# The product of a normalised tile's sum with a row, in two steps of 512 columns, with the power to -1/2 issued between them

## The chip, the cores and the metric

The kernel runs on one core of a Trainium2 chip. Its engines run side by side, each through a list of instructions of its own in order: PE multiplies matrices (PEld is its weight load), ACT evaluates functions and copies, DVE and POOL work element by element, SP and POOL also issue DMAs. The metric is the device time of one execution in microseconds (us), from timed runs; the median of three runs of the kernel before is 1109.74 us.

## What is computed

The reference is a backbone of two layers over 512 tokens of width 1024. Layer 0 is windowed attention over 16 heads with 256 context tokens, layer 1 a chunked gMLP; each is followed by a SwiGLU network with 2816 hidden columns. Both sub-layers are wrapped in the same way, and that wrapping is where the change lies:

```
def rmsnorm(x, g):
    y = x * rsqrt(mean(x * x, axis=-1) + 1e-6)
    return y * g

def modulate(h, shift, scale):
    return h * (1 + scale) + shift

h = modulate(rmsnorm(x, norm_g[i, 0]), sh_m, sc_m)
y = mixer_i(h)                                   # attention (i = 0) or gMLP (i = 1)
x = x + g_m * rmsnorm(y, norm_g[i, 1])
f = swiglu(modulate(rmsnorm(x, norm_g[i, 2]), sh_f, sc_f))
x = x + g_f * rmsnorm(f, norm_g[i, 3])
```

The last two lines of one sub-layer and the first of the next are one piece of work for each tile of 128 tokens: normalise the product y, add it to x, normalise the new x, scale and shift it, and turn it so that the next product can take it as an operand.

## The kernel before

All of x (512 tokens) stays in SBUF as four tiles of 128 tokens; c0, c1, c2 and c3 below are these tiles and the objects that carry them (`Chain`). A product in full precision is three matmuls: each operand is split into a high part (a cast on ACT, L216) and a low part (a subtraction on DVE, L223).

`down` (L1193 on) is a **seam**: it finishes the product of one sub-layer for the four tiles in turn and starts the next sub-layer's product (its head). There are three seams of this kind. Seam 1 lies between attention and the first SwiGLU network (about 255 to 300 us of the profile), seam 2 between that network and the gMLP (600 to 640), seam 3 between the gMLP and the second network (745 to 790). In seam 1 the tiles c2 and c3 carry a part of the sum in SBUF (`y_part`), so `merge` adds it, and their `gain_y` reads SBUF alone.

For each tile the steps are, with engine and line of the profile:

| step | what it does | engine, line |
|---|---|---|
| square_y, rstd_y | mean square of y; add 1e-6 on DVE, power to -1/2 on POOL (`ry`) | ACT L243, DVE L252/L250, POOL L253 |
| gain_y | tmp = y * G | DVE L1149 |
| add_x | x = tmp * ry + x, 1024 columns | DVE L1153 |
| square_x, rstd_x | mean square of x; the power of it (`rx`) | ACT L243, DVE L250, POOL L253 |
| gain_x | right half of tmp = x * row, 1024 columns | POOL L1165 |
| shift_x z | tmp = tmp * rx + row, 512 columns, z = 0, 1 | DVE L1169 |
| turn z | four transposes of 128x128 into PSUM (`hT`) | PE L1176 |
| turned_hi, turned_lo | high and low part of the turned half, into H | ACT L216, DVE L223 |

Right behind the transposes PE runs the head's matmuls (`fa` at seams 1 and 3, `v` at seam 2). In seams 1 and 3 POOL also computes sums of weights (`T`, L1408) and DVE sums of activations (`a_sum`, L1377) that the SwiGLU network needs a little later.

**What sets the order.** Every step is registered by `at(time, step, ...)`. `run_plan` sorts the steps by their place in the table ORDER (L41 to L199), a list of step names, and calls them in that order, which fixes the order of the instructions on each engine's queue. A step that is not in the table is placed by its `time`. So a change of the table moves instructions, and an engine whose next instruction has to wait holds back all that stands behind it in its list.

`rstd_of` (L247) is a DVE addition followed by the power on POOL; POOL executes it in its own order, so a power that stands behind a gain_x waits for it.

Of the kernel before, what the change touches and what calls it, by code (L numbers as in the profile page):

```python
# [11 lines left out]
ALU = mybir.AluOpType  # L12
# [3 lines left out]
D = 1024  # L16
# [25 lines left out]
x_fetch_5 x_fetch_4 square_in_4 x_fetch_1 warm_0 rstd_in_4 warm_1 dma dma#2 square_in_5 square_in_1 warm_2 warm_3  # L42
rstd_in_5 wfetch_0_0 rstd_in_1 x_fetch_2 norm_in_4_0 norm_in_5_1 norm_in_1_0 turn_in_4_0 square_in_2 norm_in_1_1
turn_in_1_0 warm_4 x_fetch_0 x_fetch_3 square_in_0 turn_in_5_1 norm_in_5_0 rstd_in_2 norm_in_2_0 turn_in_5_0
ada0_fetch_0 turned_in_4_0 square_in_3 rstd_in_0 turn_in_1_1 turned_in_5_0 turned_in_1_0 ada0_rows_0 turn_in_2_0
# [3 lines left out]
wlow_0_0 turned_in_2_0 ada0_fetch_4 ada0_cols_1 turned_in_0_0 turned_in_3_0 ada0_rows_2 modulate0_0 wfetch_1 dma#5  # L49
kv_0_4 modulated_high_0 turned_in_2_1 ada0_rows_out_2 modulated_low_0 ada0_cols_2 kv_0_2 dma#4 kv_0_3 ada0_done_1  # L50
modulated_high_1 modulate0_ctx_1 kv_0_5 ada0_done_2 modulate0_1 modulated_ctx_1 whigh_0_1 modulated_low_1 ada0_fetch_6
ada0_rows_3 norm_in_4_1 turn_in_4_1 m2start ada0_rows_out_3 turned_in_4_1 modulate0_ctx_2 kv_1_2 kv_1_4 kv_1_5
turned_in_0_1 modulated_high_2 ada0_cols_3 modulate0_2 modulated_ctx_2 kv_0_0 modulated_low_2 ada0_fetch_5 whigh_1_0
wlow_0_1 ada0_rows_4 wfetch_2 wlow_1_0 whigh_1_1 ada0_done_3 kv_1_3 kv_2_4 ada0_fetch_7 kv_2_5 modulate0_3
ada0_rows_out_4 modulated_high_3 kv_1_0 kv_0_1 kv_2_3 kv_1_1 modulate0_ctx_3 modulated_ctx_3 ada0_cols_4 ada0_done_4
modulated_high_4 ada0_rows_6 kv_3_4 wlow_1_1 ada0_rows_5 modulated_low_3 ada0_rows_out_5 m2fetch_0 modulate0_ctx_4
modulated_ctx_4 kv_2_0 kv_2_2 m2fetch_1 ada0_cols_5 modulate0_4 <lambda>#2 ada0_done_5 kv_3_2 modulated_low_4
whigh_2_0 kv_2_1 kv_3_0 ada0_rows_out_6 kv_3_5 kv_4_0 m2fetch_2 ada0_cols_6 modulated_high_5 kv_4_4 ada0_rows_7
wlow_2_0 ada0_rows_out_7 modulate0_ctx_5 whigh_2_1 kv_3_3 kv_3_1 modulate0_5 ada0_done_6 kv_4_3 m2add_0 q_first_0_0_0
m2add_1 q_first_0_0_1 kv_4_1 modulated_low_5 kv_4_2 kv_4_5 ada0_cols_7 wlow_2_1 modulate0_6 q_first_0_0_2 m2fetch_3  # L60
kv_5_2 modulated_high_6 modulated_low_6 kv_5_0 modulated_ctx_5 kv_6_2 q_first_0_0_3 q_first_0_0_4 dma#3 ada0_done_7
modulate0_7 q_first_0_0_5 kv_5_3 kv_5_1 m2add_2 kv_6_0 modulated_high_7 kv_5_4 kv_5_5 m2add_3 kv_6_1 modulate0_ctx_6
m2add_4 modulated_low_7 m2add_5 modulated_ctx_6 q_first_0_0_6 kv_7_0 modulate0_ctx_7 modulated_ctx_7 kv_6_3 kv_7_1
kv_7_2 wfetch_3 kv_7_3 kv_6_4 q_first_0_0_7 q_first_0_1_0 kv_6_5 q_first_0_1_1 q_first_0_1_2 kv_7_4 m2add_6
q_first_0_1_3 q_first_0_1_4 q_first_0_1_5 m2add_7 k_copy_0 q_first_0_1_6 m2fold q_first_0_1_7 q_first_1_0_0 v_copy_0
k_copy_2 table_Exp kv_7_5 k_rope_2 whigh_3_0 q_first_1_0_1 q_first_1_0_2 k_rope_0 m2mirror v_copy_4 k_add_2
q_first_1_0_3 k_turn_2 q_first_1_0_4 q_first_1_0_5 k_add_0 wlow_3_0_0_512 k_copy_4 k_turn_0 q_first_1_0_6
q_first_rows_0 k_split_2_0 v_copy_2 wlow_3_0_512_1024 whigh_3_1 q_next_q_mults_0 q_first_1_0_7 q_first_1_1_0
k_split_0_0 <lambda>_0 wlow_3_1_0_512 wlow_3_1_512_1024 q_next_q_split_0 q_first_1_1_1 k_turn_4 q_first_1_1_2
q_first_1_1_3 k_split_0_1 q_first_1_1_4 q_first_1_1_5 q_first_1_1_6 q_turns_0_0_bankA k_split_4_0 q_first_1_1_7  # L70
k_split_2_1 q_turns_0_1_bankA q_copy_0_0 q_first_rows_1 k_split_4_1 q_copy_0_1 block_0 q_step_2_0 q_step_2_1
q_step_2_2 m4fetch_0 score_0_0 q_step_2_3 bound_0_0 exp_0_0 score_0_1 q_step_2_4 m2fetch_gain score_0_2 q_step_2_5
bound_0_1 score_0_3 q_step_2_6 q_step_2_7 exp_0_1 q_next_q_mults_1 block_1 score_1_0 bound_0_2 bound_0_3 exp_0_2
<lambda>_1 exp_0_3 sink_0 bound_1_0 m4start total_0 q_step_2_8 q_step_2_9 score_1_1 normalise_0_3 wfetch_4 q_step_2_10
bound_1_1 q_step_2_11 q_step_2_12 q_next_q_split_1 score_1_2 q_turns_1_0_bank_t block_2 bound_1_2 score_1_3 m3start
normalise_0_1 exp_1_0 exp_1_1 q_step_2_13 q_step_2_14 bound_1_3 q_step_2_15 q_turns_1_1_bank_t q_copy_1_0 score_2_1
q_step_3_0 normalise_0_2 m4add_0 exp_1_2 q_next_q_rows_2 q_step_3_1 block_3 whigh_4_0 exp_1_3 q_step_3_2 normalise_0_0
turn_0_0 q_step_3_3 q_step_3_4 score_2_0 wlow_4_0_0_512 q_step_3_5 wfetch_5 turn_0_1 sink_1 q_copy_1_1 q_step_3_6
q_step_3_7 q_next_q_mults_2 q_step_3_8 score_2_2 total_1 turn_0_2 m2stack q_step_3_9 bound_2_1 bound_2_0 q_step_3_10
# [123 lines left out]
def backbone_kernel(ctx: ExitStack, tc: tile.TileContext, a, out):  # L203
    nc = tc.nc
# [416 lines left out]
    for t in range(NT):  # L621
        b = (3.6, 5, 6.5, 8)[t]
# [4 lines left out]
        for h in range(2):  # L627
            b = (6.4, 7.9, 9.5, 11)[t] + .45 * h
# [1426 lines left out]
```

## Time and profile before

| what | value |
|---|---|
| median of the three timed runs | 1109.74 us (1109.18 to 1111.7) |
| the profiled execution's own time | 1110.8 us |
| its span, first to last instruction | 1109.0 us |
| granted clock of TensorE | 0.998 of full |
| PEld busy | 954.6 us (86%) |
| DVE busy | 946.9 us (85%) |
| ACT busy | 613.7 us (55%) |
| POOL busy | 256.7 us (23%) |
| DVE busy in 270 to 280, 280 to 290, 290 to 300 us (seam 1) | 9.92, 9.51, 9.33 us of 10 |
| POOL busy in the same stretches | 7.58, 7.90, 9.61 us of 10 |

In rows of the timeline the columns are the start in us, the duration in us, engine, line, operation, output and inputs with their shapes, the count of instructions merged into the row, and in brackets how long the engine had stood idle before and what ended that. The duration of a row runs from when the engine takes the instruction to its end, so it holds a wait for something that the engine needs inside the instruction. The rows of waits give, for an instruction and what released it, the sum in us, how often, and the longest.

### The profile page before, as it was taken

Reading aid. Unit: us, or ns where it says so; the run is one execution under the profiler, and the core shown is the slowest. Engines: PE = TensorE matmul, PEld = TensorE weight load, DVE = VectorE, ACT = ScalarE, POOL = GpSimd, SP = SyncE. Lnnn points to the kernel's source line nnn. Section 1 sums busy time; section 2 is a strip of 40 time slices with the busy share of each in tenths; the row PEclk is TensorE's granted clock in tenths of the full one; section 3 lists DMA queues with packets and bytes.
Section 4 is the critical chain, followed back from the end, with each engine's and each line's share of the span. In section 5 each row is a group of like instructions: output and inputs, shape, how many; then the busy total and the mean of one; then the engine's idle time right before and its main releaser. Section 6 shows DMA issues by size and latency. Waiting matters only on the chain.

```text
span 1109.0 us, 17873 instructions
## 1 busy us (share of the span) xinstructions
PE 1087.6 (98%) x6974; PEld 954.6 (86%) x6974; DVE 946.9 (85%) x1418; ACT 613.7 (55%) x1060; POOL 256.7 (23%) x276
## 2 busy tenths in 40 slices
PE   7999999999999999999999999999999999999997
PEld 4688877778899999998888788888999999998876
DVE  5788988968999999987987777878988888879985
ACT  6456678756655555545665534337555545546652
POOL 1516585533700000001320511006400000002400
PEclk9999999999999999999999999999999999999999
DMA  9642433143245646449963296662133343369911
GB/s 360 266 151 89 169 95 115 64 147 114 85 151 183 210 163 198 170 136 319 239 125 116 74 330 227 203 203 82 68 132 126 134 152 123 126 223 319 167 32 76
DMA packets 48856, 179.15 MB, mean 162 GB/s; under 512 B 4858, under 2 KB 9210, under 8 KB 37636
## 3 DMA queue, kind: packets, MB, share of 16 engines
q1 hardware_dynamic: 41220, 163.34, 42.4%
q0 software_dynamic: 7552, 14.68, 7.7%
q8 instruction: 54, 0.88, 0.3%
q14 instruction: 30, 0.25, 0.1%
HBM read 171.71 MB, written 2.10 MB: 157 GB/s over the span
## 4 chain that ended last, share of the span: by engine, by line
PE 86%; DVE 7%; POOL 2%; issue 2%; DMA 1%; ACT 1%; SPq 0%; DVEq 0%; POOLq 0%; ACTq 0%
PE f L1448 35%; PE y L1632 13%; PE y L280 7%; PE y L1659 4%; PE v L280 4%; PE o_ps L957 3%; PE s_ps L904 3%; PE pT_ps L937 2%; PE u L1868 1%; PE u L1866 1%; PE u L1867 1%; DVE w_lo L223 1%; PE q_ps L272 1%; PE q_ps L274 1%; PE q_ps L273 1%
## 5 line engine op out<-in xcount | busy, mean ns | idle before, releaser
L1448 PE MATMUL f<-H,w_hi 128*128 128x256 f32 x960 | 178.6, 284 | 1.1 <-DVE fc L1459 0.5
L1448 PEld LDWEIGHTS f<-H,w_hi 128*128 128x128 f32 x960 | 149.7, 192 | 2.3 <-DVE fc L1459 1.4
L1448 PE MATMUL f<-H,w_lo 128*128 128x256 f32 x480 | 135.8, 283 | 0.0
L1632 PE MATMUL y<-w_hi,s 128*128 128x512 f32 x448 | 120.1, 389 | 0.0
L1448 PE MATMUL f<-S,w_hi 128*128 128x256 f32 x640 | 118.6, 283 | 0.0
L216 ACT CAST w_hi<-w_raw 128x1024 fp32r<-128x1024 f32 x90 | 94.6, 1053 | 34.9 <-PE y L1632 11.9
L216 ACT CAST w_hi<-T 128x1024 fp32r<-128x1024 f32 x80 | 83.6, 1047 | 52.4 <-PE f L1448 33.7
L1455 ACT COPY fc<-f 128x256 f32<-128x256 f32 x120 | 44.8, 373 | 105.7 <-PE f L1448 102.6
L223 DVE TENSOR_TENSOR w_lo<-w_raw,w_hi 128x1024 fp32r<-128x1024 f32 (+1 forms) x81 | 96.4, 1195 | 6.7 <-ACT w_hi L216 6.7
L1448 PEld LDWEIGHTS f<-S,w_hi 128*128 128x128 f32 x640 | 99.9, 192 | 0.0
L1632 PEld LDWEIGHTS y<-w_hi,s 128*128 128x128 f32 x448 | 84.1, 188 | 17.4
L223 DVE TENSOR_TENSOR w_lo<-T,w_hi 128x1024 fp32r<-128x1024 f32 x80 | 97.3, 1217 | 0.0
L1448 PEld LDWEIGHTS f<-H,w_lo 128*128 128x128 f32 x480 | 92.1, 192 | 0.0
L1448 PE MATMUL f<-S,w_lo 128*128 128x256 f32 x320 | 90.7, 284 | 0.5 <-DVE w_lo L223 0.5
L1620 POOL DMA_DIRECT2D t<-in_w x48 | 42.3, 939 | 184.3 <-DMA t<-in_w 117.2
L396 POOL DMA_DIRECT2D acc<-acc x8 | 6.9, 865 | 312.6 <-DVE acc L382 308.8
L382 DVE SCALAR_TENSOR_TENSOR acc<-ada_k,sc,acc 128x1024 f32<-128x1024 f32 x56 | 71.6, 1279 | 8.6 <-DMA ada_k<-in_ada 6.6
L1632 PE MATMUL y<-w_lo,s 128*128 128x512 f32 x224 | 69.1, 390 | 0.6 <-DVE w_lo L223 0.6
L1448 PE MATMUL f<-H,x 128*128 128x256 f32 x480 | 64.3, 283 | 0.0
L931 POOL TENSOR_SCALAR p<-p,st 128x512 f32<-128x512 f32 (+1 forms) x64 | 53.3, 848 | 43.8 <-DVE st L927 11.9
L280 PE MATMUL y<-w_hi,st 128*128 128x512 f32 x224 | 62.3, 391 | 0.0
L1448 PEld LDWEIGHTS f<-S,w_lo 128*128 128x128 f32 x320 | 61.4, 192 | 0.9 <-DVE w_lo L223 0.9
(255 smaller groups left out, 2856.5 us busy)
## 6 DMA issues: line engine op xcount, KB each, us to landing
w_raw<-in_w SPq DMA_DIRECT2D x67, 1024.0 KB, 5.1
ada_k<-in_ada SPq DMA_DIRECT2D x56, 512.0 KB, 5.2
ada_raw<-in_ada SPq DMA_DIRECT2D x12, 1024.0 KB, 4.9
w<-in_w SPq DMA_DIRECT2D x12, 1024.0 KB
t<-in_w POOLq DMA_DIRECT2D x48, 256.0 KB, 5.7
ada<-in_ada SPq DMA_DIRECT2D x8, 1024.0 KB, 8.8
t<-in_w SPq DMA_DIRECT2D x8, 1024.0 KB, 10.1
w_raw<-in_w SPq DMA_DIRECT2D x10, 512.0 KB, 5.7
```

The source lines that it names most:

```text
L216: nc.scalar.copy(out=hi, in_=src)
L223: (eng or nc.vector).tensor_tensor(out=v(lo), in0=v(src), in1=v(hi).bitcast(F32), op=ALU.subtract)
L280: nc.tensor.matmul(dst, l, w[:, n * 512:(n + 1) * 512], start=first and i == 0, stop=last and i == 2)
L382: nc.vector.scalar_tensor_tensor(out=self.acc, in0=self.raws.pop(k), scalar=sc[:, k:k + 1], in1=self.acc, op0=ALU.mult, op1=ALU.add)
L904: nc.tensor.matmul(dst, self.qT[:, j, :], keys, start=i == 0, stop=i == 1)
L931: nc.gpsimd.tensor_scalar(out=p, in0=p, scalar1=self.st[:, 12 + j:13 + j], scalar2=1.0, op0=ALU.mult, op1=ALU.mult)
L957: nc.tensor.matmul(self.o[z * HD:(z + 1) * HD, c], v, pt[:, c], start=i < 2, stop=i >= self.nb - 2, tile_position=(0, z * HD), skip_group_ ...
L1448: nc.tensor.matmul(dst, l[:, w], r[:, k, :], start=first and k == 0 and j == 0, stop=k == 3 and j == 2, skip_group_check=True)
L1455: nc.scalar.copy(out=self.c[n][:, i * 256:(i + 1) * 256], in_=self.ps[n, 1 if i == 1 else 0])
L1620: nc.gpsimd.dma_start(out=self.tt[:, p * D + 512 * i:p * D + 512 * (i + 1)], in_=a["w"][F2[self.layer] + 1 + 2 * p + i][:, c:c + 512], acc ...
L1632: nc.tensor.matmul(self.bank7(i, j), st[:, c:c + P], w[:, z * 512:(z + 1) * 512], start=i == 1 and p == 0 and l == 0 and z == 0, stop=p == ...
L1659: nc.tensor.matmul(self.y[t][n], st[:, x + t * P:x + (t + 1) * P], parts[h][w][:, n * 512:(n + 1) * 512], start=v == 0 and h == 0 and i == ...
```

## The change

`gain_x` takes a half z and multiplies 512 columns; the seam registers it twice, and the power of `rstd_x` has a time between the two:

```
-        def gain_x(self):
-            nc.gpsimd.tensor_tensor(out=self.tmp[:, D:], in0=x[:, self.t, :], in1=self.nxt[0], op=ALU.mult)
+        def gain_x(self, z):
+            for c in range(z * 512, (z + 1) * 512, 512):
+                nc.gpsimd.tensor_tensor(out=self.tmp[:, D + c:D + c + 512], in0=x[:, self.t, c:c + 512],
+                                        in1=self.nxt[0][:, c:c + 512], op=ALU.mult)
...
             at(b + 3.2, c.square_x)
-            at(b + 4.35, c.gain_x)
+            for z in range(2):
+                at(b + 4.35 + .1 * z, c.gain_x, z)
             at(b + 4.4, c.rstd_x)
```

The table ORDER is written anew: the twelve names of gain_x become twenty-four, and several dozen other names stand elsewhere, at the start of the kernel, in the attention and in the three seams. Some of its lines:

```
-c2gain_y#3 c0turn_1#3 c0turn_0#3 c1gain_x#3 c1square_x#3 c1rstd_x#3 c2rstd_y#3 wfetch_57 c1shift_x_1#3 c0turned_hi_0#3
...
+c0square_x#3 wlow_56_0 c0rstd_x#3 c0gain_x_0#3 m3done_512#2 m3done_0#2 c1rstd_y#3 c1gain_y#3 work_3_2#2 c2square_y#3
+c0shift_x_1#3 c0shift_x_0#3 c1add_x#3 c0turn_0#3 c2gain_y#3 c0turn_1#3 c1gain_x_0#3 c1gain_x_1#3 c1square_x#3
(#3 marks the third seam.) The instruction lists that come of it, at three places:

**POOL, seam 3**, tiles c0 to c3 before. `tmp_7885`, `tmp_7926`, `tmp_7932` and `tmp_8009` are the tmp of c0, c1, c2 and c3; `rx` and `ry` are their powers.

```order
L1165 TENSOR_TENSOR tmp_7885<-x_2841,row_7449 128x1024
L253 TENSOR_TENSOR rx_7900<-rx_7900,mhalf_58 128x1
L253 TENSOR_TENSOR ry_7923<-ry_7923,mhalf_58 128x1
L1165 TENSOR_TENSOR tmp_7926<-x_2841,row_7449 128x1024
L253 TENSOR_TENSOR rx_7949<-rx_7949,mhalf_58 128x1
L253 TENSOR_TENSOR ry_7952<-ry_7952,mhalf_58 128x1
L1165 TENSOR_TENSOR tmp_7932<-x_2841,row_7449 128x1024
L253 TENSOR_TENSOR ry_8006<-ry_8006,mhalf_58 128x1
L253 TENSOR_TENSOR rx_8017<-rx_8017,mhalf_58 128x1
L1165 TENSOR_TENSOR tmp_8009<-x_2841,row_7449 128x1024
```

The same stretch now (`tmp_7893`, `tmp_7917`, `tmp_7946` and `tmp_8019` are c0 to c3):

```order
L1168 TENSOR_TENSOR tmp_7893<-x_2841,row_7457 128x512
L255 TENSOR_TENSOR rx_7908<-rx_7908,mhalf_58 128x1
L1168 TENSOR_TENSOR tmp_7893<-x_2841,row_7457 128x512
L255 TENSOR_TENSOR ry_7914<-ry_7914,mhalf_58 128x1
L1168 TENSOR_TENSOR tmp_7917<-x_2841,row_7457 128x512 x2
L255 TENSOR_TENSOR rx_7959<-rx_7959,mhalf_58 128x1
L255 TENSOR_TENSOR ry_7962<-ry_7962,mhalf_58 128x1
L1168 TENSOR_TENSOR tmp_7946<-x_2841,row_7457 128x512
L255 TENSOR_TENSOR ry_8016<-ry_8016,mhalf_58 128x1
L255 TENSOR_TENSOR rx_8027<-rx_8027,mhalf_58 128x1
L1168 TENSOR_TENSOR tmp_7946<-x_2841,row_7457 128x512
L1168 TENSOR_TENSOR tmp_8019<-x_2841,row_7457 128x512
```

For c0 and c2 (and c3) the power stands between the halves; for c1 both halves stand ahead of it. Over the three seams the power stands between the halves in seven tiles (c2 and c3 of seam 1, c0 and c3 of seam 2, c0, c2 and c3 of seam 3) and behind both in five. In c0 of seam 2 the power stood ahead of the whole gain before.

**DVE, seam 3**, the end of tile c1's work and the add_x of c2, before:

```order
L1169 SCALAR_TENSOR_TENSOR tmp_7926<-tmp_7926,rx_7949,row_7773 128x512 x2
L1153 SCALAR_TENSOR_TENSOR x_2841<-tmp_7932,ry_7952,x_2841 128x1024
L223 TENSOR_TENSOR H_7595<-hT_7940,H_7595 128x4x128
L223 TENSOR_TENSOR H_7595<-hT_7935,H_7595 128x4x128
L252 TENSOR_SCALAR ry_8006<-msy_7989,msy_7992 128x1
```

and now:

```order
L1173 SCALAR_TENSOR_TENSOR tmp_7917<-tmp_7917,rx_7959,row_7781 128x512 x2
L225 TENSOR_TENSOR H_7603<-hT_7949,H_7603 128x4x128
L225 TENSOR_TENSOR H_7603<-hT_7941,H_7603 128x4x128
L1155 SCALAR_TENSOR_TENSOR x_2841<-tmp_7946,ry_7962,x_2841 128x1024
L254 TENSOR_SCALAR ry_8016<-msy_8000,msy_8003 128x1
```

The two low parts of c0's H have moved ahead of c2's add_x.

**PE, seam 1**, where tile c1 is turned, before (`hT_3147` and `hT_3174` are its two halves, `fa` the head's product for tile c0, in three groups of four matmuls):

```order
L1176 MATMUL hT_3147<-ident_65,tmp_3060 128x128 x4
L272 MATMUL fa_3161<-w_lent_2949,H_2849 128x512
L273 MATMUL fa_3161<-w_lent_2949,H_2849 128x512
L274 MATMUL fa_3161<-w_lent_2949,H_2849 128x512
```

and now:

```order
L1180 MATMUL hT_3149<-ident_65,tmp_3061 128x128 x4
L1180 MATMUL hT_3164<-ident_65,tmp_3061 128x128 x4
L274 MATMUL fa_3180<-w_lent_2949,H_2849 128x512
L275 MATMUL fa_3180<-w_lent_2949,H_2849 128x512
```

The second half's transposes have moved ahead of the twelve matmuls of the head that stood between the halves.

More of the change, by code (lines that the diff above doesn't have):

```diff
@@ L58 @@
[L58 to L67, printed above, removed]
```

288 lines of the change are left out of this document (150 added, 138 removed).

## The prediction

> **What bounds the kernel.** I read the page first, then what PE waits for, then the timeline of each seam.
>
> ```profile
> PE 1087.6 (98%) x6974; PEld 954.6 (86%) x6974; DVE 946.9 (85%) x1418; ACT 613.7 (55%) x1060; POOL 256.7 (23%) x276
> ...
> PE xT L503 <- DVE xin L480: 3.8, 3, 2.5
> ...
> PE hT L1176 <- DVE tmp L1169: 1.5, 3, 1.1
> ...
> PE f L1448 <- DVE w_lo L223: 0.5, 1, 0.5
> ```
>
> PE is busy for 1087.6 of the 1109.0 us span, so the kernel is bound by it, and only its 21.4 us of idle time can be saved. Of these the seams hold little: 1.5 us in three waits for the shifted tile (the longest 1.1), 0.5 us for the low part of a weight just behind seam 1. The change can therefore gain at most 2 us at the seams; what it can lose is not bounded so, since every step that makes PE wait anew is added in full.
>
> **The price of a half.** The whole gain, and a product of 512 columns on POOL:
>
> ```profile
> L1165 POOL TENSOR_TENSOR tmp<-x,row x12: 2387/2412/3323, 263.2 to 770.6; 128x1024 f32<-128x1024 f32 x12
> ...
> 288.34 1.29 POOL L1408 TENSOR_TENSOR T<-w_raw 128x512 f32<-128x512 f32 x1
> ```
>
> 2.39 us for 1024 columns (the shortest of twelve) and 1.29 us for 512: two halves take 2.58, 0.19 us more than the whole. In the five tiles in which the power stands behind both halves, the power comes 0.2 us later; in the seven in which it stands between, it could come 1.1 us earlier. The Trainium skill (GPSIMD Engine Reference, "Performance versus the Vector engine") has about 2.6 cycles per element at 1.2 GHz with two inputs; an estimate from that is 1.11 us for 512 without a start, so two halves would cost no more than the whole. The row decides against it, and the sum would move by under 0.2 us in a tile.
>
> **What the second half meets.** The decisive view is the timeline where POOL and DVE work at once (seam 1):
>
> ```profile
> 269.85 2.41 POOL L1165 TENSOR_TENSOR tmp<-x,row 128x1024 f32<-128x1024 f32 x1 [2.28 <-DVE x L1153]
> 271.06 2.28 DVE L1149 TENSOR_TENSOR tmp<-y_part,row 128x1024 f32<-128x1024 f32 x1
> 272.23 1.53 POOL L253 TENSOR_TENSOR rx<-rx,mhalf 128x1 f32<-128x1 f32 x1
> ...
> 280.10 1.21 DVE L1149 TENSOR_TENSOR tmp<-y_part,row 128x1024 f32<-128x1024 f32 x1
> ...
> 286.07 0.69 DVE L223 TENSOR_TENSOR H<-hT,H 128x512 fp32r<-128x512 f32 x1
> ...
> 287.32 1.05 POOL L253 TENSOR_TENSOR rx<-rx,mhalf 128x1 f32<-128x1 f32 x1
> 288.40 1.78 DVE L1169 SCALAR_TENSOR_TENSOR tmp<-tmp,rx,row 128x512 f32<-128x512 f32 x1 [0.44 <-POOL rx L253]
> ...
> 297.90 2.39 DVE L1377 TENSOR_TENSOR a_sum<-a_sum 128x512 f32<-128x512 f32 x2
> 297.96 1.79 POOL L1408 TENSOR_TENSOR T<-w_raw,T 128x512 f32<-128x512 f32 x1
> ```
>
> DVE's gain_y of c2 (`y_part`, both inputs in SBUF) is taken at 271.06 while POOL's gain runs to 272.2, and lasts 2.28 us; the same operation alone at 280.10 lasts 1.21. So DVE stood 1.07 us until POOL's instruction was over, and POOL's power, next in its list, then stood until DVE's was over: 1.53 us instead of 0.54. A low part read from PSUM (286.07) lasts 0.69 in the midst of a POOL gain and is not held. At 297.9 two DVE and one POOL instruction alternate: 0.5 us of POOL's 1.79 is a wait, and the second DVE one waits for POOL in turn. I read from it that the engines take turns, whole instruction by whole instruction, whenever DVE reads two inputs in SBUF. The Trainium skill (GPSIMD Engine Reference, "Key points") says the same of the cause: POOL shares its SBUF interfaces with VectorE, in contention with DVE instructions that have two SBUF inputs. By that rule every shift, add_x and low part of a weight is exposed, and the sum below stands; the trace agrees, with 2.28 against 1.21 us.
>
> The pair at 287.32 and 288.40 is the pattern that the change makes. A power ends at 288.37, POOL's next instruction (`T`, 288.34) starts at once, and the shift that waited for that power comes 0.06 us too late: it takes 1.78 us instead of the 0.74 of the row at 275.79 below; `T` ends at 289.63, so 0.55 us are left from there to its end. **With the power between the halves, the second half is that next instruction.** The first shift then ends at 1.29 (half) + 0.54 (power, row 610.12 below) + 1.29 (second half) + 0.55 = 3.67 us behind the start of the gain; with the whole gain it was 2.39 + 0.54 + 0.05 + 0.74 = 3.72. The early power buys nothing, and DVE is blocked while it waits.
>
> **Seam 3, tile c0 and c2: +1.9 us.**
>
> ```profile
> 752.93 3.17 POOL L1165 TENSOR_TENSOR tmp<-x,row 128x1024 f32<-128x1024 f32 x1 [2.17 <-DVE x L1153]
> ...
> 756.64 1.42 DVE L1169 SCALAR_TENSOR_TENSOR tmp<-tmp,rx,row 128x512 f32<-128x512 f32 x2 [0.65 <-POOL rx L253]
> 757.60 1.17 PE L1176 MATMUL hT<-ident,tmp 128*128 128x128 f32 x8
> ...
> 763.70 1.28 DVE L1153 SCALAR_TENSOR_TENSOR x<-tmp,ry,x 128x1024 f32<-128x1024 f32 x1
> 764.08 1.03 PE L1176 MATMUL hT<-ident,tmp 128*128 128x128 f32 x8
> ...
> 764.90 1.28 DVE L223 TENSOR_TENSOR H<-hT,H 128x512 fp32r<-128x512 f32 x2
> ...
> 769.13 1.28 DVE L1153 SCALAR_TENSOR_TENSOR x<-tmp,ry,x 128x1024 f32<-128x1024 f32 x1 [0.44 <-POOL ry L253]
> ...
> 770.33 0.74 DVE L1169 SCALAR_TENSOR_TENSOR tmp<-tmp,rx,row 128x512 f32<-128x512 f32 x1
> ...
> 771.13 0.66 PE L1176 MATMUL hT<-ident,tmp 128*128 128x128 f32 x4 [0.20 <-DVE tmp L1169]
> ```
>
> c0: the gain starts in effect at 753.8 (3.17 less 2.39 behind 752.93; DVE holds it until then). Halves 753.8 to 755.1 and, behind the power, 755.65 to 756.95. Shift 1 could go at 756.0, is held to 756.95, ends at 757.5; shift 0 ends at 758.2. PE now turns half 0 first, and comes at 757.6 as before: it stands for 0.6 us, where it stood 0.14. Call that +0.6 (0 if DVE gets in between, +1.0 if the power of c1 comes between the shifts).
> c2: its add_x now stands behind two low parts (1.28 us, row 764.90) and starts near 765.4 instead of 763.70, 1.7 later. From there: first half 766.8 to 768.1, the power of c3 held by a low part of a weight (1.21, row 278.90 below) to 769.7, c2's power to 770.2, second half; c3's add_x 769.75 to 771.0 (0.6 late), one low part that now stands ahead (0.6), then shift 0, held by the next POOL half: it ends at 772.8 to 773.4 instead of 771.07. PE comes at 771.5 (771.13 less the 0.20 in its bracket, and 0.6 from c0) and waits 1.3 to 1.9. Together PE is 1.7 to 2.3 us late at this turn; I take 1.9. Nothing later gives it back: PE waits nowhere behind 771 in this seam. Without any holding it would be +0.2.
>
> **Seam 2, tiles c0 and c1: +0.5 us.**
>
> ```profile
> 607.62 2.36 DVE L223 TENSOR_TENSOR w_lent<-w_raw,w_lent 128x1024 fp32r<-128x1024 f32 x2
> ...
> 610.12 0.54 POOL L253 TENSOR_TENSOR rx<-rx,mhalf 128x1 f32<-128x1 f32 x1 [3.74 <-DVE rx L250]
> ...
> 613.06 1.42 DVE L1169 SCALAR_TENSOR_TENSOR tmp<-tmp,rx,row 128x512 f32<-128x512 f32 x2 [1.71 <-POOL tmp L1165]
> ...
> 614.39 1.28 DVE L1153 SCALAR_TENSOR_TENSOR x<-tmp,ry,x 128x1024 f32<-128x1024 f32 x1
> ...
> 615.75 2.41 POOL L1165 TENSOR_TENSOR tmp<-x,row 128x1024 f32<-128x1024 f32 x1 [2.21 <-DVE x L1153]
> ...
> 618.70 1.42 DVE L1169 SCALAR_TENSOR_TENSOR tmp<-tmp,rx,row 128x512 f32<-128x512 f32 x2 [1.39 <-POOL rx L253]
> ...
> 619.51 1.32 PE L1176 MATMUL hT<-ident,tmp 128*128 128x128 f32 x8 [1.09 <-DVE tmp L1169]
> ```
>
> Here is the one real wait, 1.09 us before c1's turn. Before, c0's gain stood behind its power (610.12) and DVE had the two low parts at 607.62 to itself. Now the first half is there at 607.8 and takes its turn between the two (608.8 to 610.1), which moves the second low part, c1's gain_y, the power and the second half back by about 1.3 us. DVE has 1.71 us to spare at 613.06, so shift 0 comes 0.3 us late (613.35), c1's add_x too, then two halves instead of a whole (+0.2): c1's turn stands at 620.05 instead of 619.51. If POOL's half instead waited behind both low parts or passed without harm, shift 0 would start at 612.0, add_x end 1.05 us earlier, and the turn come at 618.65 (c1's square on ACT, held by c2's, then sets it): -0.86. I take +0.5, by the alternation at 297.9; both ends stay.
>
> **Seam 1: +1.2 us.**
>
> ```profile
> 275.58 0.60 PE L1176 MATMUL hT<-ident,tmp 128*128 128x128 f32 x4
> ...
> 275.79 0.74 DVE L1169 SCALAR_TENSOR_TENSOR tmp<-tmp,rx,row 128x512 f32<-128x512 f32 x1
> ...
> 278.90 1.21 DVE L223 TENSOR_TENSOR w_lent<-w_raw,w_lent 128x1024 fp32r<-128x1024 f32 x1
> ...
> 281.23 1.41 DVE L1169 SCALAR_TENSOR_TENSOR tmp<-tmp,rx,row 128x512 f32<-128x512 f32 x2
> ...
> 282.03 1.32 PE L1176 MATMUL hT<-ident,tmp 128*128 128x128 f32 x8
> ...
> 292.03 1.06 PE L1176 MATMUL hT<-ident,tmp 128*128 128x128 f32 x8 [0.20 <-DVE tmp L1169]
> ```
>
> PE turns c1's second half now right behind the first (276.2), but its shift ended at 276.53, and ends later: gain_y of c2 gets in between the two halves, so the power of c1 ends at 274.35 instead of 273.76 and the shift at 277.05. PE stands 0.85 us where the head's matmuls covered it. Then c2: its second half (278.9 to 280.2) holds the low part of a weight that DVE takes at 279.4 (278.90 before), and c2's shifts end 1.2 us later than at 282.64; PE's turn of c2, which already waits for them, is late by 1.2, the 0.85 included. If that one collision fails to come about, 0.7 us of old waits (0.20 at 292.03, 0.5 for the weight) swallow most of the 0.85; if c3's shift is held by `T` for longer than the 1.0 us of today, it is 1.9. So 0.2 to 1.9, and I take 1.2.
>
> **Start and attention: -0.6 us.**
>
> ```profile
> 28.72 0.95 DVE L480 TENSOR_SCALAR xin<-xin,r 128x512 f32<-128x512 f32 x1
> ...
> 29.81 0.63 PE L503 MATMUL xT<-ident,xin 128*128 128x128 f32 x4 [0.98 <-DVE xin L480]
> ```
>
> PE waits 0.98 us at 29.81 for a normalisation that now stands one low part (0.68) earlier on DVE, and one product fills a gap of about 0.6 near 23; an earlier reduction on DVE holds another low part 0.5 us. I take -0.6 (from -1.0 to +0.4). The fetch of the mask moves up on SP's queue past a fetch that waits for its buffer anyway: nothing. In the attention some matmuls and softmax steps swap places without a new input being late: 0, within 0.5 either way.
>
> **Sum.** 1.9 + 0.5 + 1.2 - 0.6 = +3.0 us: the profiled span of 1109.0 becomes 1112.0, its own time of 1110.8 becomes 1113.8, and the median, which lies 1.06 below that, 1109.74 + 3.0 = 1112.7 us. Its own range is 1110.5 to 1114.5.
>
> **Rivals.** *The split works* (0.18): DVE's shift gets in ahead of the second half, or the low parts lose nothing. For it: the shift needs only one half, and POOL may start slower than its row says; against it: row 288.40. Then seam 2 gains 0.86, seam 1 0.2, seam 3 loses 0.2, and the start gains 0.6: -1.5, that is 1108.2 us. This is the other side. *It does nothing* (0.15): five tiles have both halves ahead of the power, so there the change doesn't do what it says, and the collisions fall into PE's cover as most of them do today (a gain of 3.32 us, the longest in its row above, made PE wait nowhere): 1110.2, half a microsecond over today. *The stalls add up* (0.12): c3's shift in seam 1 is held by `T` (1.9), and DVE, at 9.3 to 9.9 of 10 there, cannot catch up; seam 3 at 2.5, seam 2 at 0.9: 1109.74 + 5.3 = 1115.0. The forecast has the other 0.55.
>
> **Chances.** A measurement tells 0.2% (2.2 us) from no change, so faster is below 1107.5 and slower above 1112.0. Of the forecast's 0.55 some 0.14 lies below 1112.0; of the working split 0.07 is faster. Faster 0.07, same 0.14 + 0.11 + 0.15 = 0.40, slower 0.41 + 0.12 = 0.53. The range from 1108.4 to 1115.2 leaves out about half of the working split and the worst of the stalls, 2 in 10.
>
> **What would show it.** In the profile after: halves of 1.29 us when alone; a shift of over 1 us right behind a power in seam 3's c0, c2, c3; PE waits for `hT` of about 0.9 us near 276, 1.6 before c1's turn of seam 2, and 0.6 and over 1 us in seam 3; the power of c1 in seam 1 ending later than before. I am wrong if the shifts behind a power keep 0.74 us, if PE's wait at c1's turn of seam 2 shrinks below 0.5 us, or if PE's waits for `hT` sum to under 2 us.

## The result, and the profile after

The changed kernel took 1112.8 us in the median of 10 runs (1112.0 to 1116.86), the kernel before 1110.32 us (10 runs). The ratio is 1.0031, with a 95% interval from 1.0022 to 1.0039: 3.4 us slower, 2.4 to 4.3. (The ratio goes by all runs, whose means are 1113.6 and 1110.2; the medians differ by 2.5 us.) The profiled execution took 1112.24 us, with a span of 1110.5 us (before: 1110.8 and 1109.0).

From the page, from PE's waits and from the groups of instructions on the tile `tmp` (count, then ns minimum/median/maximum, then first and last start), after:

```profile
PE 1087.8 (98%) x6974; PEld 955.3 (86%) x6974; DVE 947.7 (85%) x1418; ACT 613.5 (55%) x1060; POOL 259.9 (23%) x288
...
PE hT L1180 <- DVE tmp L1173: 3.3, 4, 1.3
PE xT L505 <- DVE xin L482: 1.7, 2, 1.4
...
L1168 POOL TENSOR_TENSOR tmp<-x,row x24: 1285/1302/2330, 262.9 to 774.1; 128x512 f32<-128x512 f32 x24
L1173 DVE SCALAR_TENSOR_TENSOR tmp<-tmp,rx,row x24: 740/749/1786, 266.9 to 776.2; 128x512 f32<-128x512 f32 x24
```

A half alone takes 1.29 to 1.30 us, as forecast; the longest, 2.33 us, is one that was held. PE's waits for the shifted tile have grown from 1.5 us to 3.3. Where they stand shows PE's timeline (start, duration, in brackets the idle time before):

```profile
276.56 0.63 PE L1180 MATMUL hT<-ident,tmp 128*128 128x128 f32 x4 [0.94 <-DVE tmp L1173]
...
292.65 1.06 PE L1180 MATMUL hT<-ident,tmp 128*128 128x128 f32 x8 [0.29 <-DVE tmp L1173]
...
386.09 0.50 PE L1453 MATMUL f<-H,w_hi 128*128 128x256 f32 x2 [0.55 <-DVE fc L1464]
...
620.72 1.32 PE L1180 MATMUL hT<-ident,tmp 128*128 128x128 f32 x8 [1.28 <-DVE tmp L1173]
...
772.55 0.66 PE L1180 MATMUL hT<-ident,tmp 128*128 128x128 f32 x4 [0.82 <-DVE tmp L1173]
```

The same matmuls stood at 292.03, 619.51 and 771.13 before, so the kernel is 0.62, 1.21 and 1.42 us late there: the program loses time step by step, and none of it is given back. The wait near 276 is new, that near 772 was 0.20.

These starts mix what a seam loses with what the start of the kernel had gained. A table by stage separates them: PE's busy time in four stretches (span, then PE busy), one from the beginning and one around each seam. PE's work is the same in both kernels, so what is missing in a stretch was stood. Before:

```profile
0.00:36.00 36.00, 27.91 (x181) 16.67 (x182) 23.04 (x59) 22.19 (x37) 10.59 (x19) 1.00 0.92 361
252.00:318.00 66.00, 65.33 (x366) 56.06 (x365) 60.99 (x83) 39.46 (x69) 30.79 (x21) 1.00 0.33 111
600.00:642.00 42.00, 40.62 (x193) 32.95 (x192) 32.86 (x48) 21.86 (x40) 15.79 (x13) 1.00 0.32 108
744.00:810.00 66.00, 65.70 (x382) 56.63 (x381) 59.07 (x86) 41.04 (x72) 30.82 (x21) 1.00 0.27 90
```

and after:

```profile
0.00:36.00 36.00, 29.29 (x184) 17.50 (x185) 23.59 (x60) 22.63 (x38) 11.68 (x20) 1.00 0.95 374
252.00:318.00 66.00, 64.30 (x358) 54.99 (x358) 60.52 (x82) 38.66 (x67) 31.46 (x25) 1.00 0.32 108
600.00:642.00 42.00, 40.41 (x190) 32.49 (x190) 35.75 (x48) 21.91 (x41) 17.32 (x17) 1.00 0.27 91
744.00:810.00 66.00, 65.13 (x377) 56.78 (x376) 58.82 (x83) 40.76 (x72) 32.02 (x25) 1.00 0.27 92
```

The tables show a gain of 1.38 us at the start (29.29 less 27.91) and losses of 1.03 (65.33 less 64.30), 0.21 and 0.57 us in the seams. In the following tables "lost" is this difference for each seam, for one profiled execution each, and "timed" the ratio's distance from 1 times the median of the kernel before, with its interval.

### The profile page after: what moved, and what is told of

The parts are those of the page before. It is cut to its first block, busy times and chain, and to the rows that moved or that the text cites. A ratio compares the mean times of both kernels' runs of the same rounds, so it can differ in the third digit from the quotient of the medians.

```text
span 1110.5 us, 17893 instructions
## 1 busy us (share of the span) xinstructions
PE 1087.8 (98%) x6974; PEld 955.3 (86%) x6974; DVE 947.7 (85%) x1418; ACT 613.5 (55%) x1060; POOL 259.9 (23%) x288
## 4 chain that ended last, share of the span: by engine, by line
PE 81%; DVE 9%; POOL 3%; issue 2%; ACT 2%; DMA 1%; SPq 0%; POOLq 0%; DVEq 0%; ACTq 0%
PE f L1453 34%; PE y L1637 13%; PE y L282 4%; PE y L1664 4%; PE v L282 3%; PE o_ps L959 3%; PE s_ps L906 3%; PE pT_ps L939 2%; POOL tmp L1168 1%; DVE w_lo L225 1%; PE u L1873 1%; PE u L1871 1%; PE u L1872 1%; DVE tmp L1173 1%; PE q_ps L274 1%
## 5 line engine op out<-in xcount | busy, mean ns | idle before, releaser
L1453 PE MATMUL f<-H,w_hi 128*128 128x256 f32 x960 | 178.6, 284 | 1.6 <-DVE fc L1464 1.1
L1453 PEld LDWEIGHTS f<-H,w_hi 128*128 128x128 f32 x960 | 149.8, 192 | 2.8 <-DVE fc L1464 1.8
L1453 PE MATMUL f<-H,w_lo 128*128 128x256 f32 x480 | 135.8, 283 | 0.0
L1453 PE MATMUL f<-S,w_hi 128*128 128x256 f32 x640 | 118.6, 283 | 0.0
L225 DVE TENSOR_TENSOR w_lo<-w_raw,w_hi 128x1024 fp32r<-128x1024 f32 (+1 forms) x81 | 96.8, 1200 | 6.7 <-ACT w_hi L218 6.7
L1453 PEld LDWEIGHTS f<-S,w_hi 128*128 128x128 f32 x640 | 99.9, 192 | 0.0
L225 DVE TENSOR_TENSOR w_lo<-T,w_hi 128x1024 fp32r<-128x1024 f32 x80 | 97.4, 1217 | 0.0
L1453 PEld LDWEIGHTS f<-H,w_lo 128*128 128x128 f32 x480 | 92.1, 192 | 0.0
L1453 PE MATMUL f<-S,w_lo 128*128 128x256 f32 x320 | 90.7, 284 | 0.5 <-DVE w_lo L225 0.5
L1453 PE MATMUL f<-H,x 128*128 128x256 f32 x480 | 64.3, 283 | 0.0
L1453 PEld LDWEIGHTS f<-S,w_lo 128*128 128x128 f32 x320 | 61.4, 192 | 0.9 <-DVE w_lo L225 0.9
```

Of the source, the lines that this page charges most:

```text
L225: (eng or nc.vector).tensor_tensor(out=v(lo), in0=v(src), in1=v(hi).bitcast(F32), op=ALU.subtract)
L1453: nc.tensor.matmul(dst, l[:, w], r[:, k, :], start=first and k == 0 and j == 0, stop=k == 3 and j == 2, skip_group_check=True)
```

## The experiments

Eleven runs. All do the same work on PE; they differ in the table of order, and order_only, start_only and the three lent runs have the whole product of 1024 columns.

| run | median us | timed against before, us | lost in seam 1, 2, 3, us |
|---|---|---|---|
| changed kernel | 1112.8 | +3.4 (2.4 to 4.3) | 1.03, 0.21, 0.57 |
| again | 1112.84 | +3.1 (2.0 to 4.2) | 1.41, 0.23, 1.22 |
| split_only | 1111.67 | +1.4 (0.6 to 2.4) | 0.42, 0.14, 0.51 |
| order_only | 1115.81 | +6.4 (5.0 to 7.9) | 0.40, 1.26, 3.08 |
| start_only | 1110.15 | +0.3 (-0.7 to 1.3) | 0.13, -0.04, -0.04 |
| head_back | 1112.03 | +2.0 (1.0 to 3.0) | 0.78, 0.22, 1.27 |
| low_back | 1111.82 | +1.8 (0.8 to 2.8) | 1.42, 0.19, 0.86 |
| three_back | 1112.38 | +2.6 (1.6 to 3.6) | 0.90, 0.31, 0.67 |
| shift_back | 1112.64 | +2.4 (1.4 to 3.3) | 1.43, 0.22, 1.34 |
| lent_late | 1110.9 | +0.9 (-0.1 to 1.9) | 0.30, 0.63, -0.12 |
| lent_behind | 1110.45 | +0.3 (-0.7 to 1.3) | 0.27, 0.45, 0.00 |
| lent_last | 1111.1 | +1.1 (0.1 to 2.1) | 0.33, 0.54, 0.03 |

**again**: the changed kernel unaltered.

> The changed kernel once more, unaltered. Its first profile lies only 1.4 us above that of the kernel before (place by place: 0.5 ahead when seam 1 begins, then 1.2 lost in seam 1, 0.4 at 386, 0.15 in seam 2, 0.2 in seam 3), while the timed medians differ by 2.5 and the ratio by 3.4. If the losses are fixed by the program, the same waits come back within 0.1 us (0.94 near 276, 1.28 near 620, 0.82 near 772) and the time is 2 to 3.5 us over the kernel before. If the waits are drawn anew in each execution, other ones appear, and the terms of one profile cannot be summed to the timed difference.

Ratio 1.0028 (1.0018 to 1.0038). The places come back (1.28 near 276, 1.29 near 620, 1.34 near 772), their sizes not all: seam 3 cost 1.22 us, 0.57 in the first profile. The wait of 0.55 us at 386 did not come back, so it is no part of the change. Why seam 3 differs within one program can be read on DVE and POOL. After, in the first profile:

```profile
768.28 0.56 POOL L255 TENSOR_TENSOR ry<-ry,mhalf 128x1 f32<-128x1 f32 x1
...
768.39 1.21 DVE L225 TENSOR_TENSOR w_lent<-w_raw,w_lent 128x1024 fp32r<-128x1024 f32 x1
768.80 1.21 POOL L255 TENSOR_TENSOR rx<-rx,mhalf 128x1 f32<-128x1 f32 x1
...
771.32 1.18 DVE L1173 SCALAR_TENSOR_TENSOR tmp<-tmp,rx,row 128x512 f32<-128x512 f32 x1
```

and in this run:

```profile
768.45 1.22 DVE L224 TENSOR_TENSOR w_lent<-w_raw,w_lent 128x1024 fp32r<-128x1024 f32 x1
768.51 1.56 POOL L254 TENSOR_TENSOR ry<-ry,mhalf 128x1 f32<-128x1 f32 x1
...
771.91 1.17 DVE L1172 SCALAR_TENSOR_TENSOR tmp<-tmp,rx,row 128x512 f32<-128x512 f32 x1
...
773.14 0.66 PE L1179 MATMUL hT<-ident,tmp 128*128 128x128 f32 x4 [1.34 <-DVE rx L251]
```

In the first, POOL's power of c3 is taken 0.11 us ahead of DVE's low part of a weight and lasts 0.56; in the second it comes 0.06 us behind it and lasts 1.56. c3's add_x, which waits for it, and with it c2's shift come 0.6 us later. Which of the two is first is decided by a tenth of a microsecond. (The bracket names the mean `rx`; the shift ahead of it ends at 773.08 and is what PE waits for.)

**split_only**: the old order, every gain in two halves at the place of the whole.

```diff
-c0gain_x
+c0gain_x_0 c0gain_x_1
...
```

> The order of the kernel before, with each gain cut into two halves of 512 columns at the place of the whole; no other step moves, and the power stands behind both halves in all twelve tiles but seam 2's c0, where it stands ahead of both. If the halves cost only their 0.19 us, c1's turn in seam 2 comes 0.2 to 0.4 later and all else stays in PE's cover: +0.4 us, 0 to +0.8. Rival, the cut itself makes the collisions (a VectorE instruction gets in between the halves and the power then waits for the next): +1.5 us or more, and the wait near 276 or 772 is there without any other move.

Ratio 1.0013 (1.0005 to 1.0022). The cut alone costs 0.42, 0.14 and 0.51 us in the seams. That is above the expected 0.4: c1's turn in seam 2 is late by 0.2 as expected, but c2's turn near 282 now waits 0.33 and c0's near 759 0.27 us. Of the first of these little is the cut's: in the three lent runs below, whose seam 1 is that of the kernel before, that turn waited 0.27 to 0.32 us and the seam lost 0.27 to 0.33, so that some 0.3 us of any figure of seam 1 is scatter. The loss in the seams is below the rival's 1.5, and the wait near 276 does not come with it, nor does the one near 772 grow beyond 0.27; the timed 1.4 lies close to the rival.

**order_only**: the new order, and the whole product of 1024 columns at the place of its first half.

```diff
-c0gain_x_1#2
+c0gain_x#2
...
-c0gain_x_0#2
...
```

> The order of the changed kernel with the whole product of 1024 columns at the place of its first half; the power stands behind it everywhere. If the losses in the seams come from the steps that were moved around the split (in seam 1 the turn of c1's second half ahead of the head's matmuls, in seam 3 low parts ahead of add_x), the wait near 276 stays, 0.2 to 0.9, and with 0.5 gained before seam 1 the time is +0.5 to +1.5 us. If the split makes them, these waits are gone and the time is at or below the kernel before: -1.0 to 0.

Ratio 1.0058 (1.0045 to 1.0071): worse than both expectations. The new order costs 6.4 us with whole products and 3.1 to 3.4 with halves, so in that order the split saves 3 us. Two places show how. In seam 2, the two low parts of a weight with a POOL product between them, order_only:

```profile
607.75 4.56 DVE L223 TENSOR_TENSOR w_lent<-w_raw,w_lent 128x1024 fp32r<-128x1024 f32 x2
607.91 3.31 POOL L1165 TENSOR_TENSOR tmp<-x,row 128x1024 f32<-128x1024 f32 x1 [1.40 <-DVE x L1153]
```

and after:

```profile
608.69 3.45 DVE L225 TENSOR_TENSOR w_lent<-w_raw,w_lent 128x1024 fp32r<-128x1024 f32 x2
608.86 2.20 POOL L1168 TENSOR_TENSOR tmp<-x,row 128x512 f32<-128x512 f32 x1 [1.40 <-DVE x L1155]
```

Alone the two take 2.36 us. A half between them costs 1.09 us, a whole 2.20, near the 1.29 and 2.41 of those products. In seam 3, order_only:

```profile
771.58 2.35 POOL L1165 TENSOR_TENSOR tmp<-x,row 128x1024 f32<-128x1024 f32 x1 [0.95 <-DVE x L1153]
771.95 2.52 DVE L1169 SCALAR_TENSOR_TENSOR tmp<-tmp,rx,row 128x512 f32<-128x512 f32 x1
...
774.53 1.11 PE L1176 MATMUL hT<-ident,tmp 128*128 128x128 f32 x4 [3.34 <-DVE rx L250]
```

c2's shift of 0.74 us lasts 2.52 behind c3's whole product, 1.18 behind a half. What the split buys is a shorter stay in the other engine's way, not an earlier power.

Not every seam gains by the split. In seam 1 the new order loses 0.40 us with whole products, and 1.03 and 1.41 with halves; near 276 PE waits 0.38 us with whole products, as the first expectation had it. The split saves in seams 2 and 3 (1.26 and 3.08 us lost without it).

That the earlier power buys nothing can be read at c3 in seam 2, where both kernels work alike except for the split. After:

```profile
630.44 1.30 POOL L1168 TENSOR_TENSOR tmp<-x,row 128x512 f32<-128x512 f32 x1 [1.46 <-DVE x L1155]
631.80 0.55 POOL L255 TENSOR_TENSOR rx<-rx,mhalf 128x1 f32<-128x1 f32 x1
632.32 1.30 POOL L1168 TENSOR_TENSOR tmp<-x,row 128x512 f32<-128x512 f32 x1
632.39 2.44 DVE L1173 SCALAR_TENSOR_TENSOR tmp<-tmp,rx,row 128x512 f32<-128x512 f32 x2 [0.67 <-POOL rx L255]
```

and order_only:

```profile
629.62 2.41 POOL L1165 TENSOR_TENSOR tmp<-x,row 128x1024 f32<-128x1024 f32 x1 [1.46 <-DVE x L1153]
631.98 0.56 POOL L253 TENSOR_TENSOR rx<-rx,mhalf 128x1 f32<-128x1 f32 x1
632.57 1.41 DVE L1169 SCALAR_TENSOR_TENSOR tmp<-tmp,rx,row 128x512 f32<-128x512 f32 x2 [1.67 <-POOL rx L253]
```

With halves the power ends 1.91 us behind the product's start (632.35 less 630.44), with the whole 2.92 (632.54 less 629.62): a microsecond earlier. Yet both shifts are done 4.39 us behind that start with halves (634.83) and 4.36 with the whole (633.98). The pair of shifts took 2.44 instead of 1.41 us, its first 1.77, since that one stood until the second half was over.

**start_only**: the old kernel, whole products, with the order of the changed one up to the first seam.

```diff
-x_fetch_5 x_fetch_4 square_in_4
+x_fetch_4 x_fetch_5 square_in_4
...
```

> The kernel before with only the moves of the start and the attention, up to the first seam; whole products, seams as before. The profile of the changed kernel shows 1.4 us gained by 36 us and 0.9 of it given back in the attention, so -0.5 us here (my forecast had -0.6), and every wait of the seams as in the kernel before. If the attention takes all of it in most executions: 0. If the seams lose what comes early (a weight that lands no earlier), the wait for a low part near 305 grows by as much and the time is 0 too.

Ratio 1.0003 (0.9994 to 1.0012). The 0.5 us can neither be shown nor excluded. The profiles tell why: PE's head start at 36 us, against the profile before, varies within one order. With the old order it was 0 (before itself), 0.15 (lent_late), 0.69 (lent_behind), 1.36 (lent_last) and 1.49 us (split_only), with the new one 0.83 here and 1.09, 1.25, 1.28, 1.38, 2.20, 2.32 and 2.41 in the others. The means, 0.74 and 1.60, differ by 0.86 us, and every profile with the new order stands 0.32 to 0.34 us more between 162 and 180 us, in the attention. That leaves half a microsecond, of which the execution's own scatter is three times as much. The 1.38 us by which the first profile of the changed kernel seemed to gain are for more than half the slow start of the profile before, which lies 0.74 us under the mean of its order.

**head_back**: in seam 1 the head's first twelve matmuls between the turns of c1's halves again.

```diff
-c1turned_lo_0 f0first_half_1 c1turn_1
+c1turned_lo_0 f0first_half_1 f0head_0_0 c1turn_1
...
-c3rstd_y f0head_0_0 c3gain_y
+c3rstd_y c3gain_y
```

> The changed kernel with one step back at its old place in seam 1: the head's first twelve matmuls stand between the turns of c1's two halves again. My forecast said that the wait near 276 (0.94 and 1.28 us in two profiles) only comes first of a delay that c2's shifts have anyway, since c2's second half holds the low part of a weight (1.86 instead of 1.21 us): then the wait goes to c2's turn near 282 and 0 to 0.5 us is won. Rival, the moved turn alone is the loss: the wait is gone, c2's turn waits no more than 0.3, and 0.9 to 1.3 us are won, a time of about 1111.6.

Ratio 1.0018 (1.0009 to 1.0027). The profile of this run:

```profile
277.12 1.30 POOL L1167 TENSOR_TENSOR tmp<-x,row 128x512 f32<-128x512 f32 x1
277.12 0.60 PE L1179 MATMUL hT<-ident,tmp 128*128 128x128 f32 x4
277.63 1.86 DVE L224 TENSOR_TENSOR w_lent<-w_raw,w_lent 128x1024 fp32r<-128x1024 f32 x1
...
281.41 1.32 PE L1179 MATMUL hT<-ident,tmp 128*128 128x128 f32 x8 [0.44 <-DVE tmp L1172]
```

The turn at 277.12 does not wait any more. c2's half still holds the weight (1.86 instead of 1.21), and c2's turn waits 0.44, with 0.21 for the weight's matmul ahead of it. Seam 1 loses 0.78 us (0.90 in three_back below, which has the same order there), against 1.03, 1.41, 1.42 and 1.43 in the four profiles with the moved turn (the changed kernel twice, low_back and shift_back). So 0.1 to 0.65 us of the wait near 276 was the turn's alone, and the rest only came ahead of c2's delay. Both explanations hold in part, with the scatter of 0.3 us on both: some of the wait went to c2's turn, as forecast, and some was won.

**low_back**: in seam 3 the two low parts of c0 behind c2's add_x again.

```diff
-c0turned_lo_1#3 c0turned_lo_0#3 c2add_x#3
+c2add_x#3
...
+c0turned_lo_0#3
...
+c0turned_lo_1#3
```

> The changed kernel with seam 3's two low parts of c0 behind c2's add_x again, as in the kernel before. My forecast charged them with 1.7 us for c2's add_x and most of the 1.9 of that seam. If that is so, c2's add_x starts 1.3 us earlier, the wait near 772 (0.82 and 1.34 us) falls to 0.3 or less, and the time is 0.6 to 1.1 us below the changed kernel. Rival, the wait is made by c3's power and c2's first shift being held by the other engine, whatever stands ahead of add_x: it stays within 0.3 of what it was and nothing is won.

Ratio 1.0016 (1.0007 to 1.0025). The profile of this run:

```profile
767.32 0.55 POOL L254 TENSOR_TENSOR ry<-ry,mhalf 128x1 f32<-128x1 f32 x1
...
768.40 1.22 DVE L224 TENSOR_TENSOR w_lent<-w_raw,w_lent 128x1024 fp32r<-128x1024 f32 x1
...
772.58 0.66 PE L1179 MATMUL hT<-ident,tmp 128*128 128x128 f32 x4 [0.76 <-DVE rx L251]
```

c2's add_x started 1.25 us earlier (764.58 against 765.83 in again), and with it c2's half and the power of c3 behind that half. The power now stands 1.08 us ahead of the low part of the weight, and is not held (0.55 us); three_back shows the same (767.42, 0.55 us). With the low parts moved, the two meet within about 0.1 us: of the four profiles with that order the first shows the power ahead (0.56 us), again, head_back and shift_back show it behind (1.56, 1.56 and 1.58 us). c2's turn waits 0.76 us here and 0.81 in three_back, as in the first profile (0.82), and 1.33 to 1.34 in the three others. So the move costs nothing when the power comes first, and 0.5 to 0.6 us when it doesn't; the rival is right for the first case, and the expectation for the second in what is won, not in the wait, which stays at 0.76 and not at 0.3. This rest goes with c2's first shift, which is held behind its second half (1.19 us) wherever add_x stands. Seam 3 lost 0.86 us, with 0.34 of it new, before c0's turn. The timed loss of 1.8 us, against 3.1 and 3.4, goes the same way, but the intervals overlap.

**three_back**: the moves of head_back and low_back, and in seam 2 the first half of c0 again behind the power.

```diff
-c0add_x#2 c0gain_x_1#2
+c0add_x#2
...
-c1gain_y#2 work_10_2 c0gain_x_0#2
+c1gain_y#2 c0gain_x_1#2 work_10_2 c0gain_x_0#2
...
```

> Both of these, and in seam 2 the first half of c0's product again behind its power, as the whole was. If the three moves carry the loss, this is the split with few of its moves and comes to the time of the split alone, +1.4 us over the kernel before (0.5 to 2); the two low parts of a weight near 608 take 2.4 us for both again instead of 3.45. If the loss lies in the halves elsewhere, it stays at +2.5 to +3.4.

Ratio 1.0023 (1.0014 to 1.0032), 2.6 us; the expected +1.4 lies just outside the interval, 2.6 lies in the alternative's +2.5 to +3.4. The two low parts near 608 took 2.36 us again, as expected, but seam 2 waits 1.26 us before c1's turn, as without this move (1.28): whether that half stands between the two weights or behind the power makes no difference to c1's turn. The idea that the three moves carry the loss is missed: the seams lose 1.88 us, with the split alone 1.07.

**shift_back**: c2's first shift in seam 3 ahead of the low part again.

```diff
+c2shift_x_0#3
 f1part_high_2_2
...
-c2shift_x_0#3
 c3rstd_x#3
```

> The changed kernel with the first shift of c2 in seam 3 at its old place, ahead of the low part of c1 that it now stands behind. If the engines take turns, c2's second half is queued behind c3's add_x and goes first; the shift waits for it 1.3 us wherever it stands, lasts 1.7 to 2.0 us instead of 1.17, ends at the same time, and the wait near 772 stays at 0.8 to 1.3: 0 won, or 0.1 to 0.6 lost because the low part, read from PSUM and not held, no longer fills that time. Rival, the place behind the low part (0.68 us) is what c2's turn waits for: the shift keeps 0.74, the wait falls by 0.6 to 0.8 and so does the time.

Ratio 1.0022 (1.0013 to 1.0030). The profile of this run:

```profile
770.41 3.67 POOL L1167 TENSOR_TENSOR tmp<-x,row 128x512 f32<-128x512 f32 x2
771.15 1.77 DVE L1172 SCALAR_TENSOR_TENSOR tmp<-tmp,rx,row 128x512 f32<-128x512 f32 x1
...
772.98 0.66 PE L1179 MATMUL hT<-ident,tmp 128*128 128x128 f32 x4 [1.33 <-DVE tmp L1172]
```

The shift starts 0.76 us earlier than in again (771.91) and lasts 1.77 instead of 1.17; PE waits 1.33 and 1.34. It ends 2.5 us behind the start of the POOL row in both (772.92 less 770.41, 773.08 less 770.56): it is released by the end of c2's second half, wherever it stands. The rival, which wanted the shift at 0.74 us and the wait 0.6 shorter, falls.

**lent_late, lent_behind, lent_last**: three tries at the old wait of 1.09 us before c1's turn in seam 2, in the kernel before with whole products. One of the two low parts of a weight that stand ahead of c0's power goes to a later place, behind c2's gain_y, then behind c1's shifts, then there behind the first low part of c0.

```diff
-wlow_43_1 wlow_44_0 <lambda>_2_2
+wlow_43_1 <lambda>_2_2
...
-c1shift_x_1#2 c2add_x#2
+c1shift_x_1#2 c0turned_lo_0#2 wlow_44_0 c2add_x#2
```

(The last of the three is shown.)

> The kernel before (whole products) with one low part of a weight in seam 2 taken from ahead of c0's rx to behind c2's gain_y, where VectorE stands idle for 1.39 us. c0's power and product then start 1.2 us earlier, c1's turn, for which TensorE waits 1.09 us, comes 0.8 to 1.0 us earlier, and the time is 0.7 to 1.0 us below the kernel before. Rival, the low part is held there by c1's product of 2.41 us and pushes c1's shift back: the wait stays over 0.6 and the time is within 0.4 of the kernel before or above it.

> The kernel before (whole products) with the same low part of a weight in seam 2 moved further, behind both shifts of c1, where neither a mean nor a power of c1 stands behind it. Ahead of it c0's shift came 0.7 us earlier in the run before; if only the mean and the power queued behind the low part spoilt that, c1's turn now waits 0.1 to 0.5 instead of 1.09 us, and the time is 0.5 to 0.9 us under the kernel before. Rival, the low part now holds c2's add_x by 1.2 us and the wait comes back at c2's turn near 627, or at the weight itself: within 0.3 of the kernel before, or slower.

> The kernel before (whole products), in seam 2 the same low part of a weight behind both shifts of c1 and now also behind the first low part of c0's turned tile, which comes ahead of c2's add_x. In the run before, c1's turn waited only 0.47 instead of 1.09 us, but TensorE then waited 1.35 us for that low part of the tile. If the two waits were all that is in the way, the first stays at 0.5, the second falls to 0.2, c2's turn comes as early, and 0.5 to 0.8 us are won, near 1109.4. Rival, c2's add_x, now 0.9 us later against PE, makes PE wait at c2's turn near 626: within 0.3 of the kernel before.

Ratios 1.0008 (0.9999 to 1.0017), 1.0003 (0.9994 to 1.0012) and 1.0010 (1.0001 to 1.0019). PE's waits in seam 2 of the three, in this order:

```profile
620.07 1.32 PE L1175 MATMUL hT<-ident,tmp 128*128 128x128 f32 x8 [1.80 <-DVE tmp L1168]
```

```profile
617.89 1.32 PE L1175 MATMUL hT<-ident,tmp 128*128 128x128 f32 x8 [0.47 <-DVE tmp L1168]
...
621.49 4.83 PE L279 MATMUL v<-w_lent,H 128*128 128x512 f32 x20 [1.35 <-DVE H L222]
```

```profile
618.09 1.32 PE L1175 MATMUL hT<-ident,tmp 128*128 128x128 f32 x8 [0.48 <-DVE tmp L1168]
...
625.31 1.20 PE L279 MATMUL v<-w_lent,H 128*128 128x512 f32 x4 [1.34 <-DVE w_lent L222]
```

All three expectations of a gain fell; the times of the first two are the rivals', lent_last is slower than its rival's 0.3 (1.1, 0.1 to 2.1), and the places are the rivals' only in part. In lent_late the low part held c1's mean and power behind it, and the wait grew. In the other two c1's turn waits half as long, as expected, but 1.35 us come back at the low part of H and then, that being early, at the next weight: 1.82 us in sum both times, where the kernel before had 1.29 (1.09 and 0.20). No version that beats the kernel before came out of this.

## Why the prediction was right, point by point

It said 1112.7 us; the medians were 1112.8 and 1112.84. The mechanism, turns by whole instructions that make PE wait in the seams, is shown. That the time came within 0.1 us is luck in part: the sum stands on 1109.74, the median of three runs, where ten gave 1110.32, and it is better than its terms. None of the signs of being wrong came: shifts behind a power took up to 1.77 us, PE's wait at c1's turn of seam 2 was 1.28, and its waits for `hT` sum to 3.3.

- **The halves** at 1.29 us: right (1.285 to 1.302).
- **Turns by whole instructions, and an early power that buys nothing**: right, and the best confirmed point. c3 in seam 2 has its first shift done 3.72 us behind the start of the product with halves (forecast 3.67) and its pair at the same time as with the whole; shift_back shows the release by the half's end. The Trainium skill (GPSIMD Engine Reference, "Key points") names the shared SBUF interfaces and the case of two SBUF inputs; the runs agree, and show the size here: an instruction stands nearly as long as the other engine's lasts, 1.09 us behind a half (1.29 alone), 2.20 behind a whole (2.41).
- **The price of the cut**, 0.19 us a tile: right where nothing else happens (c1's turn in seam 2). With its collisions the cut alone is 1.4 us.
- **Seam 1, +1.2**: the size is right, 1.03 and 1.41 against the profile before, about 0.2 less against the mean of the five profiles that have the old seam 1 with whole products (0, 0.13, 0.27, 0.30, 0.33). The low part of the weight was held for 1.86 instead of 1.21 us, as forecast. The wait near 276 was 0.94 and 1.28 (forecast 0.85), and it is the moved turn's, since head_back has none; but its working failed. c1's power was to end 0.59 us later and its second shift 0.52. Measured from DVE's addition of `y_part` ahead of them (269.44 after, 269.62 before), the power ended 0.2 and the shift 0.07 us later. What fills the gap is that PE reached the turn 0.38 us (0.71 in again) further ahead of DVE than in the profile before. Profiles of the old order have such a lead too (0.35 in lent_late, 0.42 in lent_last), so it is luck that 0.85 came out near. That it is contained in c2's delay was right in part: head_back and three_back won 0.1 to 0.65.
- **Seam 2, +0.5**: right in its direction, too large; 0.21 and 0.23 measured. The two low parts did take 3.45 us with the half in between. The 0.3 us by which shift 0 was to be late did not come: it started at 614.13, and against the 613.06 of the row before that is the 1.08 us by which all of DVE was late there (605.27 against 604.19 for gain_y ahead of it). The term was the 0.2 of the cut.
- **Seam 3, +1.9**: the place is right, and the size was 0.57 in the first profile, 1.22 to 1.34 in again, head_back and shift_back. The working for c2 came as told: its add_x started at 765.61 (forecast 765.4), its first half ended at 768.33 (768.1), and in those three profiles the power of c3 was held behind the low part of the weight and PE waited 1.33 or 1.34 us (forecast 1.3 to 1.9). In the first profile the power came first, and PE waited 0.82. The sum had no such second case. The term that was mis-sized is c0's 0.6: it was 0 in both profiles of the changed kernel and 0.18 to 0.34 in head_back, low_back and shift_back.
- **Start, -0.6**: open. start_only timed +0.3 (-0.7 to 1.3), and its profiles are compatible with -0.5. **Attention, 0**: 0.32 to 0.34 lost in each profile with the new order.

The terms as measured, -0.5 with the attention, and as means of the changed kernel's two profiles 1.0, 0.2 and 0.9 in the seams, sum to +1.6 us; the timing says +3.4 (2.4 to 4.3) and +3.1 (2.0 to 4.2). Part of the gap lies in which execution was profiled. The first profile is of one of 1112.24 us, 1.35 below the mean of its ten (1113.6), which three of 1114.6 to 1116.9 raise; no profile shows where those lost their time. The profile of again (1112.81 us) lies at the mean of its fast runs (1112.9). There the seams lose 2.86 us, 0.2 of it scatter of seam 1, the start wins 0.35 against the mean of the old order, and the 0.33 lost in the attention was won ahead of it: 2.3 us, inside the interval of what was timed. What is left stays open.

Of the rivals, the working split is refuted as a whole: no seam gained. "It does nothing" fails too, by split_only's 1.4 us and by seam 1. "The stalls add up" (1115.0, a sum that leaves the start's -0.6 out) needed 1.9, 0.9 and 2.5 us in the seams; no profile of the changed kernel has more than 1.41, 0.23 and 1.22. What none of the cases had is that the new order was made bearable by the split, in seams 2 and 3: 6.4 us without it.

## What to carry to other kernels

Before an instruction is cut to let a short one in between, look at what takes its turn next: here the second piece went ahead of the very step that the short one was to release. Cutting can still pay, by halving the longest hold that the other engine's instructions meet, so judge it against the order it runs in, and the order against the cut. And before a gain at the beginning of a kernel is believed, compare several profiles of one order: here they differed by 1.5 us.

## What the runs showed of the hardware that was not expected

That a power over 128 by 1 elements is held behind DVE was known from the profile before (1.53 us instead of 0.54). Not expected was that two executions of one program differ in it: taken 0.11 us ahead of a DVE instruction with two SBUF inputs the power lasted 0.56 us, taken 0.06 us behind it 1.56. So seam 3 has two outcomes, PE waiting 0.82 or about 1.34 us. A shift of 0.74 us was drawn out to 2.52 by a whole product on POOL (order_only).
